# Hybrid streaming encoder step: weight splitting and modulation moved from GpSimd to VectorE, groups reordered, part of the modulation moved to the second feed-forward part

## The chip, the cores and the metric

The kernel runs on one core of a Trainium2 chip. The metric is the device time in microseconds of one execution of the whole program. The core's engines are TensorE (PE, with its weight loads as PEld), VectorE (DVE), ScalarE (ACT), GpSimd (POOL) and SyncE (SP), which issues all DMAs of this kernel. Each engine works through its own queue in order.

## The reference

One layer of an encoder is computed for 1024 prompt tokens and 32 sample tokens, model width 1024, feed-forward width 2816, all in float32.

```python
def layer(x, c, ...):
    mod = silu(c) @ w_mod + b_mod                    # (1024) @ (1024, 9*1024), for two c: prompt and sample
    sh1, sc1, g1, sh2, sc2, g2, sh3, sc3, g3 = split(mod, 9)
    h = rmsnorm(x, gains[0]) * (1 + sc1) + sh1
    x = x + 0.5 * g1 * rmsnorm((silu(h @ w1_gate) * (h @ w1_up)) @ w1_down, gains[1])
    h = rmsnorm(x, gains[2]) * (1 + sc2) + sh2
    qa, ka, va, qb, kb, vb = split(h @ w_in)
    o = concat([rmsnorm(band_attention_A), rmsnorm(window_attention_B)]) @ w_out
    x = x + g2 * rmsnorm(o, gains[3])
    h = rmsnorm(x, gains[4]) * (1 + sc3) + sh3
    x = x + 0.5 * g3 * rmsnorm((silu(h @ w2_gate) * (h @ w2_up)) @ w2_down, gains[5])
    return x, (new keys and values)
```

## The kernel before

**Stages.** The 1056 tokens are cut into three blocks: block 0 and block 1 of 384 tokens, block 2 of 288 (256 prompt tokens and the 32 sample tokens). The kernel runs the first feed-forward part (key `h1`, "part one"), then the projections, both attentions and the output projection, then the second feed-forward part (key `h3`, "part two"). Activations lie with the model dimension on the partitions and tokens along the free dimension.

**Precision.** Every float32 matrix product is made of three matmuls in a reduced format. `pair_of` splits a weight tile of 128 x 512: ScalarE writes the rounded copy `w[:, 0]` (line 549), another engine subtracts it from the original to get the remainder `w[:, 1]` (line 550). The three products are high x high, high x low, low x high (`product`, line 609, and `down`, lines 821 to 823).

**Groups and rounds.** The 22 slices of the feed-forward width make 11 groups of two slices. A round is one group on some of the blocks: stages gate ("g"), up ("u") and down ("d"). `rounds` lists them, and the stages are interleaved so that gate of the next round comes ahead of down of this one. In part one before, groups 0 to 7 run on all three blocks, then 8 to 10 on blocks 0 and 1, then 8 to 10 again on block 2. In part two, groups 0 and 1 run on each block by itself (six single rounds, `LEAD = 2`), then 2 to 10 on all three.

**Plain groups and block products.** A plain group (`plain`) takes 8 products of weight quarters by activation halves for blocks 0 and 1 (four per block) and four for block 2. A "fast" group (`strassen`) treats gate or up on blocks 0 and 1 as a 2 x 2 block product and needs seven products in place of eight; block 2's four products ride along with four of the weights. For this it needs sums of weight quarters, S1 to S4 (`Mat.of`, line 574, tiles `ws`), with their own splits, and combinations of the activations, T1 to T4 (`combos`, lines 620 to 655). In part one before, groups 5 to 10 on blocks 0 and 1 are fast (`PLAIN = 5`); in part two, all three-block rounds are.

**GpSimd's share.** Before, GpSimd makes S1 to S4 (`SUMS_POOL`) and the remainders of their splits. In rounds on one block ("alone", `shared`) it also makes the remainders of A12 and A22 and of the second slice of down's weights (`Rows`, lines 550 and 601).

**Modulation.** The first 16 of 72 columns of 128 are made at the start with matmuls. The rest comes in pieces of three columns (`mod_aside`): for each of eight slices of the contraction, VectorE accumulates the prompt's product (`acc[0]`, lines 250 and 252). For the sample, ScalarE scales the slice (line 253), and GpSimd adds (lines 256 and 258). At the end small matmuls with a vector of ones sum over the partitions (line 265, tile `pms`), and VectorE adds the bias and forms coefficients. A piece has eleven steps.

**Order of the work.** Side work (norms, modulation, bias rows, combinations) stands in a list of generators, and `step(n)` advances the first of them n steps: five after each product group of a plain round in part one (`STEPS`), two after each of a fast one (`pace`), one after each pair of down's outputs. `need` runs side work until a named piece is done. This gives the program order, and a scheduler with a timeline model then orders each engine's instructions with that order as priority. `per_group` is a hook that `ffn` calls after each up stage, and also after each stage of round 0 in part one; `mod_rest` uses it to begin the modulation and the bias rows. In round 0 it runs after gate and after down, so both are begun twice, one after the other:

```python
            if what == "u" or (key, r) == ("h1", 0):
                if 2 in blocks:
                    per_group(gi)
```

**Buffers.** Tiles come from pools with fixed numbers of buffers: `w` (split weights), `r` (raw weights), `s` (slices such as `sl`, `ut`, `macc`), `g`, `ux`; `FFN1` and `FFN2` list the numbers for the two parts. The pool `h` has five buffers for `ws`, for the modulation's loads `wma` and scaled slices `wmn`, and for the norms' temporaries.

Of the kernel before, what the change touches and what calls it, by code (L numbers as in the profile page):

```python
# [55 lines left out]
START = "x02nw1y3"  # L56
LEAD = 2
LAST = 3
PLAIN = 5
STEPS = {"h1": (5, 5), "h3": (6, 6)}  # L60
FFN1 = {"ux": 3, "r": 4, "w": 4, "g": 6, "s": 11}
FFN2 = {"ux": 3, "r": 4, "w": 5, "g": 6, "s": 9}
MIX = {"w": 8, "r": 3, "g": 5, "s": 5, "m": 1}
MODS = [(("ux", 6), ("r", 2))] * 4
SUMS_POOL = ("S1", "S2", "S3", "S4")
ZPOOL = (1, 0, 1, 0)
LATE = 1
PRIME = 0
# [16 lines left out]
def encoder_step(ctx: ExitStack, tc, x_prompt, x_sample, cache_a_k, cache_a_v, cache_b_k, cache_b_v,  # L85
# [152 lines left out]
    def mod_aside(c0, nc_):  # L238

        w = 128 * nc_  # L240
        acc = [s_tile([128, 384], "macc")[:, :w] for _ in range(2)]
        for g in range(4):
            r = h_tile([128, 2, 384], "wma")[:, :, :w]
            dma.dma_start(r, w_mod[0, 256 * g:256 * (g + 1), 128 * c0:128 * c0 + w]
                          .rearrange("(k p) n -> p k n", p=128))
            n = h_tile([128, 2, 384], "wmn")[:, :, :w]
            for kk in range(2):
                k = 2 * g + kk
                if k == 0:
                    ve.tensor_scalar(acc[0], r[:, kk], csil[:, k, 0:1], None, op0=OP.mult)  # L250
                else:
                    ve.scalar_tensor_tensor(acc[0], r[:, kk], csil[:, k, 0:1], acc[0], op0=OP.mult, op1=OP.add)  # L252
                ae.activation(n[:, kk], r[:, kk], AF.Copy, scale=csil[:, k, 1:2])  # L253
                if kk:
                    to = acc[1] if g == 0 else n[:, 0]
                    ge.tensor_tensor(to, n[:, 0], n[:, 1], op=OP.add)  # L256
                    if g:
                        ge.tensor_tensor(acc[1], acc[1], n[:, 0], op=OP.add)  # L258
                yield
        yield  # L260
        yield
        pm = pc("pms")[:, :2 * nc_].rearrange("p (j b) -> p j b", j=2)
        for j in range(2):
            for b in range(nc_):
                te.matmul(pm[:, j, b:b + 1], acc[j][:, 128 * b:128 * b + 128], ones, start=j == 0 and b == 0,
                          stop=j == 1 and b == nc_ - 1, skip_group_check=True)
        ve.tensor_copy(modT[:, :, c0:c0 + nc_], pm)
        coefs(c0, c0 + nc_)
        yield

    def mod_all(first):
        for c0 in range(first, 72, 3):
            yield from mod_aside(c0, min(3, 72 - c0))


    ub = {}
# [266 lines left out]
        yield from norm_h(f, tb, j + 1, H)  # L543


    def pair_of(src, tag="w", at=None, by=None):

        w = at if at is not None else t_tile(tag, [128, 2, 4, 128], "w", F32R)
        ae.activation(w[:, 0], src, AF.Copy)  # L549
        (by or ve).tensor_tensor(w[:, 1], src, w[:, 0], op=OP.subtract)  # L550
        return w[:, 0], w[:, 1]

    class Mat:


        def __init__(self, wm, gi, shared):
            self.aside = ("A12", "A22") if shared else ()
            self.r = []
            for d in range(2):
                r = t_tile("r", [128, 4, 256], "raw")  # L560
                dma.dma_start(r, wm[0, 512 * d:512 * d + 512, 256 * gi:256 * gi + 256]
                              .rearrange("(k p) n -> p k n", p=128))
                self.r.append(r)
            self.a = {f"A{f + 1}{d + 1}": self.r[d][:, :, 128 * f:128 * f + 128] for f in range(2) for d in range(2)}
            self.done, self.places = {}, []

        def of(self, name):
            a = self.a
            if name not in a:
                x, y, op = {"S1": ("A21", "A22", OP.add), "S2": ("S1", "A11", OP.subtract),  # L570
                            "S3": ("A11", "A21", OP.subtract), "S4": ("A12", "S2", OP.subtract)}[name]
                x, y = self.of(x), self.of(y)
                a[name] = h_tile([128, 4, 128], "ws")
                (ge if name in SUMS_POOL else ve).tensor_tensor(a[name], x, y, op=op)  # L574
            return a[name]

        def split(self, name):
            if name not in self.done:
                self.done[name] = pair_of(self.of(name), *(self.places.pop(0) if self.places else ()),
                                          by=ge if name[0] == "S" or name in self.aside else ve)  # L580
            return self.done[name]

    class Rows:


        def __init__(self, wm, gi, tag, shared):
            self.raw, self.w, self.tag, self.shared = [], {}, tag, shared
            for ff in (2 * gi, 2 * gi + 1):
                r = t_tile("r", [128, KT, 128], "raw")
                dma.dma_start(r, wm[0, 128 * ff:128 * ff + 128, :].rearrange("p (k n) -> p k n", n=128))  # L590
                self.raw.append(r)

        def split(self, q, hf):
            if (q, hf) in self.w:
                return
            if self.tag == "w":
                self.w[q, hf] = pair_of(self.raw[q][:, 4 * hf:4 * hf + 4], by=ge if self.shared and q else ve)
                return
            t = t_tile(self.tag, [128, 2, KT, 128], "wd", F32R)
            ae.activation(t[:, 0], self.raw[q], AF.Copy)  # L600
            (ge if self.shared and q else ve).tensor_tensor(t[:, 1], self.raw[q], t[:, 0], op=OP.subtract)
            for h in range(2):
                self.w[q, h] = t[:, 0, 4 * h:4 * h + 4], t[:, 1, 4 * h:4 * h + 4]

# [57 lines left out]
    def rounds(key):  # L662
        both, n = (0, 1, 2), NF // 2
        if key == "h3":
            return [(g, (tb,)) for tb in both for g in range(LEAD)] + [(g, both) for g in range(LEAD, n)]
        return [(g, both) for g in range(n - LAST)] + [(g, (0, 1)) for g in range(n - LAST, n)] + \
            [(g, (2,)) for g in range(n - LAST, n)]

    STRASSEN = [("A11", "B11", "a", 2), ("A12", "B21", "a", 2), ("S2", "T2", "b", 0), ("S1", "T1", "d", 0),
                ("S3", "T3", "b", 0), ("A22", "T4", "e", 2), ("A21", None, None, 2), ("S4", "B22", "d", 0)]  # L670
# [1 line left out]
    def ffn(key, H, tags, F, facc, wg, wu, wd, per_group, key_out, after, beside=lambda: None):  # L672
# [2 lines left out]
        final = {tb: max(i for i, (g, t) in enumerate(plan) if tb in t) for tb in range(3)}  # L675
        T, sl, gs, loaded = {}, {}, {}, {}
        pace = 2
        fast = {r for r, (g, t) in enumerate(plan) if len(t) == 3 and (key == "h3" or g >= PLAIN) or len(t) == 2}
        stages = []
        for r, (gi, blocks) in enumerate(plan):  # L680
            held = [stages.pop()] if r else []
# [2 lines left out]
        def load(i):  # L684
            if i >= len(stages) or stages[i] in loaded:
                return
            r, what = stages[i]
            gi, blocks = plan[r]
            alone = len(blocks) == 1
            if what == "d":  # L690
                loaded[r, what] = Rows(wd, gi, "ux" if key == "h1" and alone else "w", alone)
            else:
                loaded[r, what] = Mat((wg, wu)[what == "u"], gi, alone)

        def ready(i):

# [141 lines left out]
        yield  # L838
        if key == "h3":
            begin((key, 2), between(F2[2], 2, 1, H3))  # L840
            begin((key, "T"), combos(H, T, tags))
        for i, (r, what) in enumerate(stages):
            gi, blocks = plan[r]
            if (key, r, what) == ("h1", 0, "u"):
# [23 lines left out]
            elif r == 0 and key == "h1":  # L868
                mu = loaded[r, "u"]
                mu.places = [(None, p) for p in wide()] + [("r",)]  # L870
                for tb in blocks:
                    need((key, tb))
                    last = tb == blocks[-1]
                    plain(r, "g", m, [tb], lambda n: None)
                    plain(r, "u", mu, [tb], lambda n, last=last: nexts(n, 1, i + 1) if last else None)
            elif r in fast:
                need((key, "T"))
                strassen(r, what, m, 2 in blocks, lambda n: nexts(n, 4 if what == "g" else 5))
            else:
                for tb in blocks:  # L880
                    need((key, tb))
                if what == "g" and (key, gi) == ("h1", PLAIN - 1):
                    begin((key, "T"), combos(H, T, tags), first=True)
                plain(r, what, m, blocks, lambda n: nexts(n, 2 * len(blocks) - 1))
            if what == "u" or (key, r) == ("h1", 0):
                if 2 in blocks:
                    per_group(gi)
                if gi == NF // 2 - 1:
                    beside()

# [28 lines left out]
    F1 = [None] * 3  # L919
    H2, H3 = [None] * 3, [None] * 3  # L920

    def mod_rest(gi):
        if gi == 0:
            in_order.close()
            begin("mod", mod_all(16))
            begin("bias", bias_rows())

    ffn1 = ffn("h1", H1, (("T3", "ux"), ("T1", "u"), ("T2", "ux"), ("T4", "u")), F1, lambda tb: u_tile(tb, "facc", F32), w1_gate, w1_up, w1_down, mod_rest, "h2",
# [688 lines left out]
    def facc2(tb):  # L1617
        return u_tile(tb, "facc", F32) if tb else pools["ux"].tile([128, KT, 384], F32, name="facc", tag="ux")

    for _ in ffn("h3", H3, (("T3", "ux"), ("T1", "x"), ("T2", "ux"), ("T4", "x")), F3, facc2, w2_gate, w2_up, w2_down, lambda gi: None, "y", finale, beside):  # L1620
        pass
    finish()

# [26 lines left out]
```

## Time and profile before

| | |
|---|---|
| median of 3 runs | 2368.66 us (2366.12 to 2372.91) |
| profiled execution: time | 2369.16 us |
| profiled execution: span, first to last instruction | 2367.4 us |
| mean granted TensorE clock | 0.959 |
| part one, first gate matmul to last down matmul | 43 to 967 us |
| part two, first gate matmul to end | 1555 to 2367 us |

In the profile's rows, L550 is line 550 of the kernel; a group's row gives line, engine, operation, tiles (written <- read), shape, count, busy time, mean duration in ns, and the idle time ahead of it with what ended it. A row of windows gives start and end, width, then busy time and number of instructions of each engine, the granted clock as a share of full speed, the DMA engines' busy share and GB/s. A row of waits names who waited for whom, with the sum, the number and the longest. A row of the chain or the timeline begins with the start and the length in us.

### The profile page before, as it was taken

To read this page: it belongs to the slowest core of one execution; us is meant where nothing else is said; L and a number is where in the kernel's file an instruction comes from. 1 tells how busy PE (TensorE), PEld (TensorE's weight loads), DVE (VectorE), ACT (ScalarE), POOL (GpSimd) and SP (SyncE) were. 2 spreads that over 40 slices of the span, in tenths; PEclk is the share of its full clock that TensorE was granted. 3 is DMA by queue.
4 is the path that set the end of the run, shared out by engine and by line. 5 is a ranking of instruction groups with operands and counts; after the bars stand their busy time and mean duration, and the time that the engine had idled before them with its cause. 6 is when DMAs were issued, how large, how long until landed. Compare 5 with 4: busy or idle time off the path is not lost.

```text
span 2367.4 us, 36544 instructions
## 1 busy us (share of the span) xinstructions
PE 2197.4 (93%) x13988; PEld 2083.5 (88%) x13988; DVE 1572.6 (66%) x2891; ACT 1010.4 (43%) x2118; POOL 928.3 (39%) x850
## 2 busy tenths in 40 slices
PE   7999989998889998889999999985999999999998
PEld 4999989998888898889978768985999999999997
DVE  5688898777878658767754576678535455545548
ACT  4464433434434334447654566344442232323224
POOL 2275563566667534310011032345462333333321
PEclk8999999999999999889999989997999999999999
DMA  8355435333433334410121211152431111111114
GB/s 318 102 161 165 136 123 157 107 102 117 133 98 121 121 94 147 145 56 25 30 57 28 65 37 54 54 164 90 126 106 37 54 54 54 49 42 46 45 54 129
DMA packets 179123, 225.05 MB, mean 95 GB/s; under 512 B 10116, under 2 KB 162116, under 8 KB 177796
## 3 DMA queue, kind: packets, MB, share of 16 engines
q1 hardware_dynamic: 178948, 222.71, 30.5%
q8 instruction: 110, 1.80, 0.3%
q14 instruction: 65, 0.53, 0.1%
HBM read 202.94 MB, written 26.03 MB: 97 GB/s over the span
## 4 chain that ended last, share of the span: by engine, by line
PE 63%; DVE 19%; DMA 7%; POOL 4%; issue 3%; ACT 2%; SPq 0%; DVEq 0%; POOLq 0%; ACTq 0%
PE gu L609 7%; PE ge L609 6%; DVE macc L252 5%; PE dn L821 5%; PE dn L822 5%; PE dn L823 5%; PE up L609 5%; PE gate L609 4%; PE g L609 4%; DMA wma<-in_w_mod_dram 4%; PE po L1003 2%; PE S L1042 2%; PE pq L352 2%; DVE w L550 2%; PE pq L354 2%
## 5 line engine op out<-in xcount | busy, mean ns | idle before, releaser
L550 DVE TENSOR_TENSOR w<-raw,w 128x512 fp32r<-128x512 f32 x279 | 259.6, 933 | 211.1 <-ACT w L549 209.8
L821 PE MATMUL dn<-gg,w 128*128 128x384 f32 (+1 forms) x1008 | 335.0, 333 | 37.0 <-ACT facc L826 18.6
L549 ACT ACTIVATE w<-raw 128x512 fp32r<-128x512 f32 x327 | 202.6, 629 | 354.7 <-PE gu L609 111.4
L822 PE MATMUL dn<-gg,w 128*128 128x384 f32 (+1 forms) x1008 | 329.1, 326 | 2.0 <-DVE gg L724 2.0
L823 PE MATMUL dn<-gg,w 128*128 128x384 f32 (+1 forms) x1008 | 328.6, 326 | 0.0
L828 DVE TENSOR_TENSOR facc<-dn,facc 128x768 f32<-128x768 f32 (+1 forms) x240 | 212.1, 886 | 148.7 <-PE dn L823 148.7
L550 POOL TENSOR_TENSOR w<-ws,w 128x512 fp32r<-128x512 f32 x120 | 169.0, 1415 | 287.3 <-ACT w L549 268.7
L252 DVE SCALAR_TENSOR_TENSOR macc<-wma,csil,macc 128x384 f32<-128x384 f32 (+1 forms) x266 | 245.2, 922 | 47.2 <-DMA wma<-in_w_mod_dram 43.4
L253 ACT ACTIVATE wmn<-wma,csil 128x384 f32<-128x384 f32 (+1 forms) x304 | 168.2, 604 | 177.4 <-DMA wma<-in_w_mod_dram 135.2
L821 PEld LDWEIGHTS dn<-gg,w 128*128 128x128 f32 x1008 | 192.4, 191 | 44.7 <-DVE facc L828 19.6
L609 PE MATMUL gu<-t,w 128*128 128x384 f32 x1080 | 207.0, 343 | 9.0 <-DVE sl L769 7.7
L256 POOL TENSOR_TENSOR wmn<-wmn 128x384 f32<-128x384 f32 (+1 forms) x114 | 126.8, 1112 | 199.0 <-ACT wmn L253 172.7
L609 PEld LDWEIGHTS gu<-t,w 128*128 128x128 f32 x1080 | 192.8, 194 | 11.0 <-DVE sl L769 8.3
L822 PEld LDWEIGHTS dn<-gg,w 128*128 128x128 f32 x1008 | 192.7, 191 | 2.4 <-DVE gg L724 2.4
L823 PEld LDWEIGHTS dn<-gg,w 128*128 128x128 f32 x1008 | 192.5, 191 | 0.0
L609 PE MATMUL g<-h_hi,w 128*128 128x288 f32 x768 | 164.7, 295 | 1.3 <-DVE facc L828 1.3
L574 POOL TENSOR_TENSOR ws<-raw 128x512 f32<-128x512 f32 x60 | 88.7, 1478 | 147.6 <-DMA raw<-in_w_up_dram 77.8
L258 POOL TENSOR_TENSOR macc<-macc,wmn 128x384 f32<-128x384 f32 (+1 forms) x114 | 135.4, 1188 | 7.1
L549 ACT ACTIVATE w<-ws 128x512 fp32r<-128x512 f32 x120 | 74.0, 629 | 149.7 <-PE gu L609 56.9
L609 PE MATMUL ge<-h,w 128*128 128x384 f32 x720 | 137.9, 335 | 0.0
L609 PE MATMUL gate<-h,w 128*128 128x384 f32 x672 | 125.0, 341 | 8.5 <-DVE w L550 5.1
L609 PEld LDWEIGHTS g<-h_hi,w 128*128 128x128 f32 x768 | 127.8, 188 | 2.0 <-DVE facc L828 1.7
(301 smaller groups left out, 5237.4 us busy)
## 6 DMA issues: line engine op xcount, KB each, us to landing
wma<-in_w_mod_dram SPq DMA_DIRECT2D x144, 384.0 KB, 3.3
raw<-in_w_gate_dram SPq DMA_DIRECT2D x58, 512.0 KB, 4.1
raw<-in_w_up_dram SPq DMA_DIRECT2D x58, 512.0 KB, 4.0
raw<-in_w_down_dram SPq DMA_DIRECT2D x58, 512.0 KB, 4.3
raw<-in_w_in_dram SPq DMA_DIRECT2D x18, 512.0 KB, 4.0
raw<-in_w_out_dram SPq DMA_DIRECT2D x13, 512.0 KB, 4.3
wm<-in_w_mod_dram SPq DMA_DIRECT2D x8, 768.0 KB, 11.2
xr<-xs SPq DMA_DIRECT2D x16, 384.0 KB, 4.0
```

Source lines behind the costliest of these rows:

```text
L252: ve.scalar_tensor_tensor(acc[0], r[:, kk], csil[:, k, 0:1], acc[0], op0=OP.mult, op1=OP.add)
L253: ae.activation(n[:, kk], r[:, kk], AF.Copy, scale=csil[:, k, 1:2])
L256: ge.tensor_tensor(to, n[:, 0], n[:, 1], op=OP.add)
L258: ge.tensor_tensor(acc[1], acc[1], n[:, 0], op=OP.add)
L549: ae.activation(w[:, 0], src, AF.Copy)
L550: (by or ve).tensor_tensor(w[:, 1], src, w[:, 0], op=OP.subtract)
L574: (ge if name in SUMS_POOL else ve).tensor_tensor(a[name], x, y, op=op)
L609: te.matmul(ps, w[a][:, k, :], x[b][k], start=first and k == 0 and q == 0, stop=last and k == n - 1 and q == 2, skip_group_check=True)
L821: te.matmul(ps[:, s, :w], h[:, k % 4, :], g[:, 0, :w], start=q == 0, stop=False)
L822: te.matmul(ps[:, s, :w], h[:, k % 4, :], g[:, 1, :w], start=False, stop=False)
L823: te.matmul(ps[:, s, :w], l[:, k % 4, :], g[:, 0, :w], start=False, stop=q == 1)
L828: ve.tensor_tensor(o, ps[:, :, :w], o, op=OP.add)
```

## The change

- GpSimd no longer takes part in the splitting of weights: S1 to S4 and all remainders are made by VectorE (`SUMS_POOL`, `shared` and `by` are gone).
- In `mod_aside`, VectorE accumulates both the prompt's and the sample's products, 16 instructions a piece; ScalarE's scaling and GpSimd's additions are gone, and with them the tile `wmn`.
- Part one's rounds become: groups 0 to 2 on blocks 0 and 1, groups 3 to 10 on all blocks, then groups 0 to 2 on block 2. Groups 0 to 6 are plain (`PLAIN = 7`), 7 to 10 use block products with block 2.
- The hook is called with the round's number. Part one makes the modulation's columns 16 to 63; the last eight (the gate of part two) begin in part two after the up stage of round 6.
- In part two the combinations T1 to T4 begin with round 4, block 2's first single, and no longer at the part's start. Its pools have four `w` and eleven `s` buffers.

```diff
-PLAIN = 5
+PLAIN = 7
-FFN2 = {"ux": 3, "r": 4, "w": 5, "g": 6, "s": 9}
+FFN2 = {"ux": 3, "r": 4, "w": 4, "g": 6, "s": 11}
-SUMS_POOL = ("S1", "S2", "S3", "S4")
...
-            n = h_tile([128, 2, 384], "wmn")[:, :, :w]
             for kk in range(2):
                 k = 2 * g + kk
-                if k == 0:
-                    ve.tensor_scalar(acc[0], r[:, kk], csil[:, k, 0:1], None, op0=OP.mult)
-                else:
-                    ve.scalar_tensor_tensor(acc[0], r[:, kk], csil[:, k, 0:1], acc[0], op0=OP.mult, op1=OP.add)
-                ae.activation(n[:, kk], r[:, kk], AF.Copy, scale=csil[:, k, 1:2])
-                if kk:
-                    to = acc[1] if g == 0 else n[:, 0]
-                    ge.tensor_tensor(to, n[:, 0], n[:, 1], op=OP.add)
-                    if g:
-                        ge.tensor_tensor(acc[1], acc[1], n[:, 0], op=OP.add)
+                for j in range(2):
+                    c = csil[:, k, j:j + 1]
+                    if k == 0:
+                        ve.tensor_scalar(acc[j], r[:, kk], c, None, op0=OP.mult)
+                    else:
+                        ve.scalar_tensor_tensor(acc[j], r[:, kk], c, acc[j], op0=OP.mult, op1=OP.add)
                 yield
...
-    def mod_all(first):
-        for c0 in range(first, 72, 3):
+    def mod_all(first, last):
+        for c0 in range(first, last, 3):
...
-        (by or ve).tensor_tensor(w[:, 1], src, w[:, 0], op=OP.subtract)
+        ve.tensor_tensor(w[:, 1], src, w[:, 0], op=OP.subtract)
...
-                (ge if name in SUMS_POOL else ve).tensor_tensor(a[name], x, y, op=op)
+                ve.tensor_tensor(a[name], x, y, op=op)
...
-            (ge if self.shared and q else ve).tensor_tensor(t[:, 1], self.raw[q], t[:, 0], op=OP.subtract)
+            ve.tensor_tensor(t[:, 1], self.raw[q], t[:, 0], op=OP.subtract)
...
-        return [(g, both) for g in range(n - LAST)] + [(g, (0, 1)) for g in range(n - LAST, n)] + \
-            [(g, (2,)) for g in range(n - LAST, n)]
+        return [(g, (0, 1)) for g in range(LAST)] + [(g, both) for g in range(LAST, n)] + \
+            [(g, (2,)) for g in range(LAST)]
...
-        fast = {r for r, (g, t) in enumerate(plan) if len(t) == 3 and (key == "h3" or g >= PLAIN) or len(t) == 2}
+        fast = {r for r, (g, t) in enumerate(plan) if len(t) == 3 and (key == "h3" or g >= PLAIN)}
...
             begin((key, 2), between(F2[2], 2, 1, H3))
-            begin((key, "T"), combos(H, T, tags))
...
-                if what == "g" and (key, gi) == ("h1", PLAIN - 1):
-                    begin((key, "T"), combos(H, T, tags), first=True)
+                if what == "g" and (key, r) in (("h1", PLAIN - 1), ("h3", 2 * LEAD)):
+                    begin((key, "T"), combos(H, T, tags), first=key == "h1")
...
-                if 2 in blocks:
-                    per_group(gi)
+                per_group(r)
...
-    def mod_rest(gi):
-        if gi == 0:
+    def mod_rest(r):
+        if r == 0:
             in_order.close()
-            begin("mod", mod_all(16))
+            begin("mod", mod_all(16, 64))
             begin("bias", bias_rows())
...
+    def beside_lead(r):
+        if r == 3 * LEAD:
+            begin("mod", mod_all(64, 72))
```

More of the change, by code (lines that the diff above doesn't have):

```diff
@@ L269, in mod_aside @@
         yield
-    def mod_all(first):
-        for c0 in range(first, 72, 3):
-            yield from mod_aside(c0, min(3, 72 - c0))
+    def mod_all(first, last):
+        for c0 in range(first, last, 3):
+            yield from mod_aside(c0, min(3, last - c0))
     ub = {}
@@ L543, in between, with pair_of, __init__ @@
         yield from norm_h(f, tb, j + 1, H)
-    def pair_of(src, tag="w", at=None, by=None):
+    def pair_of(src, tag="w", at=None):
         w = at if at is not None else t_tile(tag, [128, 2, 4, 128], "w", F32R)
         ae.activation(w[:, 0], src, AF.Copy)
-        (by or ve).tensor_tensor(w[:, 1], src, w[:, 0], op=OP.subtract)
+        ve.tensor_tensor(w[:, 1], src, w[:, 0], op=OP.subtract)
         return w[:, 0], w[:, 1]
     class Mat:
-        def __init__(self, wm, gi, shared):
-            self.aside = ("A12", "A22") if shared else ()
+        def __init__(self, wm, gi):
             self.r = []
@@ L578, in split, with __init__ @@
             if name not in self.done:
-                self.done[name] = pair_of(self.of(name), *(self.places.pop(0) if self.places else ()),
-                                          by=ge if name[0] == "S" or name in self.aside else ve)
+                self.done[name] = pair_of(self.of(name), *(self.places.pop(0) if self.places else ()))
             return self.done[name]
     class Rows:
-        def __init__(self, wm, gi, tag, shared):
-            self.raw, self.w, self.tag, self.shared = [], {}, tag, shared
+        def __init__(self, wm, gi, tag):
+            self.raw, self.w, self.tag = [], {}, tag
             for ff in (2 * gi, 2 * gi + 1):
@@ L596, in split @@
             if self.tag == "w":
-                self.w[q, hf] = pair_of(self.raw[q][:, 4 * hf:4 * hf + 4], by=ge if self.shared and q else ve)
+                self.w[q, hf] = pair_of(self.raw[q][:, 4 * hf:4 * hf + 4])
                 return
@@ L688, in load @@
             gi, blocks = plan[r]
-            alone = len(blocks) == 1
             if what == "d":
-                loaded[r, what] = Rows(wd, gi, "ux" if key == "h1" and alone else "w", alone)
+                loaded[r, what] = Rows(wd, gi, "ux" if key == "h1" and len(blocks) == 1 else "w")
             else:
-                loaded[r, what] = Mat((wg, wu)[what == "u"], gi, alone)
+                loaded[r, what] = Mat((wg, wu)[what == "u"], gi)
         def ready(i):
@@ L1618, in facc2 @@
         return u_tile(tb, "facc", F32) if tb else pools["ux"].tile([128, KT, 384], F32, name="facc", tag="ux")
-    for _ in ffn("h3", H3, (("T3", "ux"), ("T1", "x"), ("T2", "ux"), ("T4", "x")), F3, facc2, w2_gate, w2_up, w2_down, lambda gi: None, "y", finale, beside):
+    def beside_lead(r):
+        if r == 3 * LEAD:
+            begin("mod", mod_all(64, 72))
+    for _ in ffn("h3", H3, (("T3", "ux"), ("T1", "x"), ("T2", "ux"), ("T4", "x")), F3, facc2, w2_gate, w2_up, w2_down, beside_lead, "y", finale, beside):
         pass
```

## The prediction

> **What bounds the kernel now.** I read the page first, then the windows by stage, then the engines' waits, then the timeline of VectorE beside GpSimd.
>
> ```profile
> PE 2197.4 (93%) x13988; PEld 2083.5 (88%) x13988; DVE 1572.6 (66%) x2891; ACT 1010.4 (43%) x2118; POOL 928.3 (39%) x850
> PEclk8999999999999999889999989997999999999999
> ```
>
> TensorE is busy 93% of 2367.4 us, so at most some 7% can be won by better feeding. The windows, cut at the ends of rounds, say where it is lost: width, then busy us of PE (with its matmuls), PEld, DVE, ACT, POOL, then clock.
>
> ```profile
> 43.00:133.00 90.00, 84.42 (x528) 82.28 (x528) 68.41 (x138) 47.94 (x99) 34.44 (x32) 0.94 0.44 139
> 133.00:171.00 38.00, 33.31 (x202) 32.79 (x201) 31.23 (x40) 22.67 (x40) 25.74 (x23) 0.96 0.53 156
> 171.00:256.00 85.00, 79.75 (x507) 77.20 (x506) 77.31 (x103) 40.81 (x77) 52.24 (x45) 1.00 0.53 161
> 256.00:345.00 89.00, 82.84 (x512) 82.05 (x512) 76.44 (x108) 39.42 (x77) 52.16 (x46) 0.94 0.46 141
> 345.00:424.00 79.00, 75.69 (x469) 74.73 (x468) 66.62 (x122) 28.01 (x52) 37.62 (x28) 0.98 0.42 126
> 424.00:503.00 79.00, 73.62 (x461) 72.42 (x459) 56.67 (x81) 32.11 (x61) 40.20 (x35) 0.98 0.35 111
> 503.00:587.00 84.00, 75.38 (x455) 73.04 (x455) 64.46 (x93) 35.07 (x66) 55.00 (x45) 0.96 0.38 113
> 587.00:671.00 84.00, 75.27 (x461) 72.96 (x459) 64.08 (x90) 35.92 (x68) 54.33 (x45) 0.96 0.38 113
> 671.00:748.00 77.00, 68.98 (x405) 67.58 (x406) 61.80 (x86) 32.18 (x61) 53.29 (x43) 0.93 0.41 125
> 748.00:810.00 62.00, 53.78 (x275) 51.70 (x274) 45.36 (x90) 20.77 (x40) 38.38 (x31) 0.89 0.43 132
> 895.00:967.00 72.00, 61.79 (x426) 60.53 (x424) 60.08 (x97) 31.41 (x52) 35.33 (x23) 0.91 0.43 144
> 1616.00:1657.00 41.00, 16.13 (x69) 15.30 (x68) 35.74 (x63) 17.69 (x37) 17.07 (x11) 0.63 0.16 54
> 1833.00:1899.00 66.00, 64.92 (x409) 64.60 (x408) 32.79 (x46) 18.21 (x35) 23.14 (x16) 1.00 0.17 49
> ```
>
> The last row is one round of block products in part two. It takes 66.0 us. The same round in part one (503 to 748) takes 77 to 84 us, and there POOL and DVE are far busier and the clock is lower. What TensorE itself needs comes from undisturbed runs of matmuls in the chain, the first on 384 columns, the second on 288, the third one modulation piece:
>
> ```profile
> 864.16 4.16 PE gu L609 x24
> 1899.26 3.19 PE g L609 x24
> 176.75 1.23 PE pms L265 x12
> ```
>
> So 0.173 us for 384 columns, 0.133 for 288, and 0.480 for one product on all three blocks. A plain round has 96 products per block for gate and up and 48 for down: 144 x 0.480 = 69.1 us. A round of block products has 168 at 0.173, 96 at 0.133 and 48 at 0.480: 64.9 (the row above: 66.0). Without block 2 it is 45.7, a plain round on blocks 0 and 1 is 49.9, block 2 alone 19.1.
>
> Part one before, 43 to 967 us: five plain rounds, three of block products, three with two blocks and three singles need 345 + 195 + 137 + 57 = 734 us, and 38 modulation pieces 47. Of 924 us about 140 are lost: near 36 up to 171 (rounds 0 and the gate of 1), 33 from 171 to 503 (four plain rounds, and 221 further matmuls, some 18 pieces: 299 needed), 40 from 503 to 748 (205 needed), 24 from 748 to 967 (195 needed).
>
> Why, the timeline of 20 us shows; DVE first, then POOL:
>
> ```profile
> 699.81 0.55 DVE L724 TENSOR_TENSOR gg<-sl,gg 128x384 fp32r<-128x384 f32 x1
> 700.28 0.61 DVE L252 SCALAR_TENSOR_TENSOR macc<-wma,csil,macc 128x384 f32<-128x384 f32 x1
> 705.22 1.49 DVE L550 TENSOR_TENSOR w<-raw,w 128x512 fp32r<-128x512 f32 x1
> 706.63 1.63 DVE L252 SCALAR_TENSOR_TENSOR macc<-wma,csil,macc 128x384 f32<-128x384 f32 x1
> 713.45 0.61 DVE L252 SCALAR_TENSOR_TENSOR macc<-wma,csil,macc 128x384 f32<-128x384 f32 x1
> 713.98 0.16 DVE L267 COPY modT<-pms 128x6 f32<-128x6 f32 x1
> 714.51 0.68 DVE L550 TENSOR_TENSOR w<-raw,w 128x512 fp32r<-128x512 f32 x1
> 715.11 1.37 DVE L252 SCALAR_TENSOR_TENSOR macc<-wma,csil,macc 128x384 f32<-128x384 f32 x1
> 717.76 0.94 DVE L828 TENSOR_TENSOR facc<-dn,facc 128x768 f32<-128x768 f32 x1
> 718.63 1.19 DVE L252 SCALAR_TENSOR_TENSOR macc<-wma,csil,macc 128x384 f32<-128x384 f32 x1
> 705.05 1.11 POOL L258 TENSOR_TENSOR macc<-macc,wmn 128x384 f32<-128x384 f32 x1
> 706.12 1.72 POOL L550 TENSOR_TENSOR w<-ws,w 128x512 fp32r<-128x512 f32 x1
> ```
>
> With POOL silent (713.45, 714.51) the accumulation takes 0.61 and the weights' remainder 0.68; beside a POOL instruction (705.22, 706.63) they take 1.49 and 1.63. Starts stand closer than durations: 0.53 us after the accumulation, 0.60 after the remainder, 0.47 after a 384-wide subtraction, 0.87 after the sum out of PSUM (717.76 to 718.63). [...]
>
> ```profile
> L252 DVE SCALAR_TENSOR_TENSOR macc<-wma,csil,macc 128x384 f32<-128x384 f32 (+1 forms) x266 | 245.2, 922 | 47.2 <-DMA wma<-in_w_mod_dram 43.4
> L253 ACT ACTIVATE wmn<-wma,csil 128x384 f32<-128x384 f32 (+1 forms) x304 | 168.2, 604 | 177.4 <-DMA wma<-in_w_mod_dram 135.2
> L258 POOL TENSOR_TENSOR macc<-macc,wmn 128x384 f32<-128x384 f32 (+1 forms) x114 | 135.4, 1188 | 7.1
> PE pms L265 <- DVE macc L252: 12.3, 5, 4.5
> PE pms L265 <- DVE macc L252: 12.0, 5, 4.2
> PE gu L609 <- POOL w L550: 6.7, 8, 1.5
> PE dn L821 <- ACT facc L826: 18.6, 2, 15.3
> ```
>
> The waits are TensorE's: the first two in 100 to 500 and 500 to 900 us, the third in the rounds of part two, the last in its lead. The 304 activations are 38 pieces of eight: the hook that starts the modulation is called twice in round 0, so every piece is made twice. After, it is 2 x 16 in part one and 3 in part two, 35.
>
> **The change, part by part.**
>
> *Matmuls of part one.* Seven plain groups (three split into two blocks and one) and four with block products need 3 x (49.9 + 19.1) + 4 x 69.1 + 4 x 64.9 = 743 us, 8 more than before. Six fewer pieces give 6 x 1.23 = 7 back, and three return in part two (+3.7). So TensorE's need stays near 782 us in part one; only the losses can move.
>
> *Modulation on VectorE.* A piece was 8 accumulations on DVE, 8 activations, 7 POOL sums; it becomes 16 DVE instructions. At a pitch of 0.53 that is 8.5 us, with the small ones 8.8. The 30 pieces that the hand-counted steps put into rounds 1 to 6 (eleven steps each; 366 steps there after those for the combinations, 36 of them for the bias rows) are 264 us. The DMA waits of 43 us should mostly go, since a piece no longer takes two of the five h buffers per load. [...]
>
> *DVE in rounds 1 to 6.* A plain round: 12 remainders x 0.60, 12 products and remainders of 0.47 (narrow ones 3/4), 12 sums of 0.87 (narrow 3/4) = 22 us; with two blocks 18. Rounds 1 to 6: 2 x 18 + 4 x 22 + 264 + combinations (20 wide instructions x 0.87, and some 8 us behind the POOL sums that stay) 25 + bias 6 = 419 us. TensorE needs there 2 x 49.9 + 4 x 69.1 + 30 x 1.23 = 413. Two queues are equally loaded, which is the weak point: it can't run at 413. Bounds: 419 with no friction; 332/299 = 1.11 of TensorE's need, as rounds 1 to 4 ran before, gives 458. DVE was busy up to 77.3 of 85 us there, 91%; 419/0.92 = 455. I take 455, a loss of 42, near the upper bound because the pieces' small matmuls still stand in TensorE's order and wait for the accumulators.
>
> *Rounds 7 to 10.* The modulation is out by the start of round 7. DVE has the 32.8 us of the 1833 row, 16 instructions more at 0.60 (10), less what POOL held up: some 40 of 65. Each takes 66.0; round 7 with two late pieces 69. Before, 171 to 748 lost 73 us; after, rounds 1 to 7 lose 42 + 2: 29 won. Rounds 8 to 10 and the singles lost 24, half of it from 748 to 810 with modulation still running; I take 15: 9 won. At the start only blocks 0 and 1 must be normed for round 0: of 36 lost I take 4 back (bounds 0 and the 14 us in which block 2's products stood there). Part one: 42 less 1.
>
> [...]
>
> *Part two.* Sums and remainders on DVE take the 6.7 us of POOL waits away. The third modulation part is 12 loads on SP's queue ahead of weights, 24 + 24 DVE instructions (25 us, covered: DVE is half idle) and 3.7 us of TensorE. The combinations start with block 2's first single instead of right behind its norm. In the 1616 row TensorE is busy 16 of 41 us, with ACT's copy out of PSUM (15.3 us wait) behind ACT's norm and combinations; the norm remains, the combinations (some 14 of the 41) move under two rounds of TensorE work of 38 us. I take 5 (bounds 0 and 14). Weights with 4 buffers instead of 5: nothing, since part one's block products ran on 4 with the waits named above; at worst each of 18 stages waits for one copy and remainder, 18 x 1.3 = 24. Sum: 3.7 - 6.7 - 5 = -8.
>
> *Sum.* The profiled execution took 2369.2 (span 2367.4), 0.5 above the median. 2369.2 - 41 - 8 = 2320.
>
> **The rivals.**
>
> *VectorE becomes the bound (slower).* Accumulations in a row that depend on each other start 0.65 us apart in the chain:
>
> ```profile
> 297.19 0.63 DVE macc L252
> 297.84 0.63 DVE macc L252
> 298.50 0.63 DVE macc L252
> ```
>
> If the two accumulators don't alternate cleanly, a piece costs 16 x 0.12 = 1.9 us more, 30 of them 58; DVE needs 477, at 92% 518, and part one's gain of 41 turns into a loss of 22: 2369.2 + 22 - 8 = 2383. It decides from a pitch of 0.62. Against it: the new loop alternates them, so each has another between. [...]
>
> *The stalls were never POOL's (same).* In-order queues lose as much without POOL, part one keeps its 924 us: 2369.2 - 6.7 + 3.7 = 2366. For it: DVE's busy time in part one hardly falls (contention out, work in). Against: the 1833 row.
>
> [...]
>
> **How the numbers follow.** Forecast 0.45, DVE-bound 0.17, same 0.13, port 0.20, something else 0.05, split. Within 0.3% (7 us, about what this kernel's runs can tell apart) lies the second rival: 0.14. Slower 0.19, faster 0.67. Range 2284 to 2374: from the third rival to short of the first, which with the unknown is left out; the forecast's own range is 2300 to 2345.
>
> **What the profile after would show.** L252 near 0.62 us mean, not 0.92, and x480 to x500; no POOL row of L256, L550 or L574 left; rounds 3 to 6 near 76 us each and 7 to 10 near 66, clock 1.00; part one's last down near 926 instead of 967. Wrong: PE's waits for macc L252 above 24 us and DVE over 95% busy in the plain rounds (first rival); rounds of 77 to 84 us with POOL silent (second); weights' waits in part two's rounds (four buffers).

## The result

The changed kernel takes 2305.15 us (median of 4 runs, 2302.55 to 2307.05) against 2369.16 (4 runs, 2366.12 to 2372.91): 64 us less, ratio 0.9728 with a 95% interval of 0.9711 to 0.9746. The forecast was 2320, with a range of 2284 to 2374. The profiled execution's span fell from 2367.4 to 2300.6 us.

The page after, first its busy shares, then the clock in forty slices:

```profile
PE 2176.9 (95%) x14004; PEld 2070.8 (90%) x14004; DVE 1611.4 (70%) x3383; ACT 843.6 (37%) x1800; POOL 214.6 (9%) x293
PEclk9999999998999998999999999999999999999999
```

VectorE is busier than before (1611 us against 1573) and executes 492 instructions more; GpSimd fell from 928 to 215 us. The groups of the modulation and of the weights after:

```profile
L252 DVE SCALAR_TENSOR_TENSOR macc<-wma,csil,macc 128x384 f32<-128x384 f32 (+1 forms) x490 | 279.6, 611 | 4.8 <-DMA wma<-in_w_mod_dram 4.8
L544 DVE TENSOR_TENSOR w<-raw,w 128x512 fp32r<-128x512 f32 x333 | 231.0, 703 | 96.2 <-ACT w L543 94.4
```

490 accumulations cost 280 us, 266 had cost 245: the mean fell from 922 to 611 ns. The waits for their loads fell from 43 to 5 us. Nine of them in a row show the distance from start to start, 4.84 less 0.61 us over eight steps, 0.53:

```profile
160.26 4.84 DVE L252 SCALAR_TENSOR_TENSOR macc<-wma,csil,macc 128x384 f32<-128x384 f32 x9
```

The windows after, cut at the ends of down's rounds; columns as before:

```profile
42.50:131.00 88.50, 82.94 (x488) 81.05 (x487) 75.63 (x175) 41.94 (x83) 13.43 (x14) 0.94 0.52 176
131.00:192.00 61.00, 60.80 (x370) 60.48 (x368) 55.55 (x115) 13.02 (x25) 0.00 (x0) 1.00 0.57 170
192.00:259.00 67.00, 65.62 (x409) 64.35 (x410) 62.96 (x131) 11.04 (x21) 0.00 (x0) 1.00 0.58 175
259.00:343.00 84.00, 79.47 (x498) 78.69 (x498) 69.33 (x168) 15.09 (x29) 0.00 (x0) 0.98 0.57 175
343.00:423.00 80.00, 77.93 (x507) 77.15 (x505) 63.80 (x133) 13.08 (x26) 0.00 (x0) 1.00 0.45 139
423.00:505.00 82.00, 76.77 (x479) 76.21 (x478) 79.25 (x128) 16.37 (x29) 15.25 (x6) 0.96 0.35 107
505.00:588.00 83.00, 78.19 (x465) 75.95 (x464) 74.26 (x178) 17.22 (x33) 0.00 (x0) 0.92 0.50 152
588.00:655.00 67.00, 65.44 (x412) 65.23 (x411) 39.11 (x63) 18.92 (x35) 0.00 (x0) 1.00 0.17 48
655.00:724.00 69.00, 66.90 (x412) 66.70 (x411) 39.16 (x63) 18.84 (x36) 0.00 (x0) 0.98 0.16 47
1887.00:1956.00 69.00, 66.59 (x410) 66.38 (x409) 39.07 (x62) 18.64 (x34) 0.00 (x0) 0.98 0.16 46
```

The plain rounds 3 to 6 take 80 to 84 us with VectorE busy up to 79 of 82; block products in part one take 67 to 69 us, and 77 to 84 before. The last row is one round of part two: it was 66.0 us before and is 69 now.

The table shows where the 67 us of span come from. The stages are cut at TensorE instructions of the timeline: part one begins with the first gate matmul, and the cuts behind it are its last down matmul, the first scores of mixer B, the first gate matmul of part two, its first block product, its last down matmul and the end.

| stage, us | before | after | difference | forecast |
|---|---|---|---|---|
| part one | 924.4 | 874.6 | -49.8 | -41 |
| from part one to the first scores | 89.2 | 78.7 | -10.5 | 0 |
| attention and output projection | 499.1 | 496.1 | -3.0 | 0 |
| part two's lead, the single rounds | 178.8 | 153.4 | -25.4 | -5 |
| part two's rounds of block products | 614.0 | 637.6 | +23.6 | -3 |
| end | 19.0 | 17.6 | -1.4 | 0 |

So the sum was near, but two of its terms were far off and stood against each other.

### The profile page after: what moved, and what is told of

It reads as the page before. It is cut to its first block, busy times and chain, and to the rows that moved or that the text cites. A ratio compares the mean times of both kernels' runs of the same rounds, so it can differ in the third digit from the quotient of the medians.

```text
span 2300.6 us, 35729 instructions
## 1 busy us (share of the span) xinstructions
PE 2176.9 (95%) x14004; PEld 2070.8 (90%) x14004; DVE 1611.4 (70%) x3383; ACT 843.6 (37%) x1800; POOL 214.6 (9%) x293
## 4 chain that ended last, share of the span: by engine, by line
PE 74%; DVE 14%; DMA 5%; issue 4%; ACT 2%; POOL 1%; SPq 1%; DVEq 0%; ACTq 0%; POOLq 0%
PE gu L601 8%; PE up L601 7%; PE gate L601 6%; PE ge L601 6%; PE dn L812 6%; PE dn L813 6%; PE dn L814 6%; PE g L601 5%; DVE w L544 3%; DVE macc L252 3%; PE po L992 2%; PE S L1031 2%; PE pq L346 2%; DMA raw<-in_w_up_dram 2%; PE pq L348 2%
## 5 line engine op out<-in xcount | busy, mean ns | idle before, releaser
L544 DVE TENSOR_TENSOR w<-raw,w 128x512 fp32r<-128x512 f32 x333 | 231.0, 703 | 96.2 <-ACT w L543 94.4
L252 DVE SCALAR_TENSOR_TENSOR macc<-wma,csil,macc 128x384 f32<-128x384 f32 (+1 forms) x490 | 279.6, 611 | 4.8 <-DMA wma<-in_w_mod_dram 4.8
L601 PE MATMUL gu<-t,w 128*128 128x384 f32 x936 | 175.3, 340 | 1.0 <-DVE w L544 1.0
L601 PE MATMUL gate<-h,w 128*128 128x384 f32 x864 | 161.7, 342 | 9.0 <-DVE w L544 7.3
L601 PEld LDWEIGHTS gate<-h,w 128*128 128x128 f32 x864 | 152.0, 191 | 11.2 <-DVE w L544 8.6
L389 POOL TENSOR_TENSOR sq<-sq 128x384 f32<-128x384 f32 (+1 forms) x48 | 52.3, 1099 | 1146.3 <-ACT sq L385 1134.2
L601 PE MATMUL up<-h,w 128*128 128x384 f32 x792 | 146.3, 337 | 1.1 <-ACT w L543 1.1
L601 PEld LDWEIGHTS up<-h,w 128*128 128x128 f32 x792 | 137.4, 189 | 2.3 <-ACT w L543 2.2
L714 ACT ACTIVATE gg<-sl 128x384 fp32r<-128x384 f32 (+1 forms) x132 | 62.4, 492 | 195.5 <-DVE sl L713 194.8
L601 PE MATMUL g<-h_lo,w 128*128 128x288 f32 x416 | 122.7, 295 | 0.0
```

The source lines that it names most:

```text
L252: ve.scalar_tensor_tensor(acc[j], r[:, kk], c, acc[j], op0=OP.mult, op1=OP.add)
L389: e.tensor_tensor(sq[:, 0, :w], sq[:, 0, :w], sq[:, 1, :w], op=OP.add)
L544: ve.tensor_tensor(w[:, 1], src, w[:, 0], op=OP.subtract)
L601: te.matmul(ps, w[a][:, k, :], x[b][k], start=first and k == 0 and q == 0, stop=last and k == n - 1 and q == 2, skip_group_check=True)
L714: ae.activation(g[:, 0, :w], v, AF.Copy)
```

## The experiments

Medians are compared with the kernel before on the same chip; the stages are those of the table above.

**The three parts alone.** Each starts from the kernel before.

```diff
# o1_mod_dve: modulation
-                ae.activation(n[:, kk], r[:, kk], AF.Copy, scale=csil[:, k, 1:2])
-                if kk: ... ge.tensor_tensor(...)
+                for j in range(2):
+                    ... ve.scalar_tensor_tensor(acc[j], r[:, kk], c, acc[j], op0=OP.mult, op1=OP.add)
# o2_weights_dve: sums and remainders of weights
-SUMS_POOL = ("S1", "S2", "S3", "S4")
+SUMS_POOL = ()
-... by=ge if name[0] == "S" or name in self.aside else ve
+... by=ve
# o3_order: part one's rounds
-PLAIN = 5
+PLAIN = 7
-        return [(g, both) for g in range(n - LAST)] + ...
+        return [(g, (0, 1)) for g in range(LAST)] + [(g, both) for g in range(LAST, n)] + [(g, (2,)) for g in range(LAST)]
... (which rounds are fast, and the hook's argument, follow as in the change)
```

Expected of the modulation alone:

> The kernel before with one part of the change: the modulation's pieces accumulate on VectorE alone (16 instructions a piece, no ScalarE scaling, no GpSimd sums). GpSimd keeps its weights; order and part two stay. Port theory (GpSimd's instructions holding VectorE are what part one loses): GpSimd's 308 us of modulation sums go, part one shortens by 25 to 40 us, L252's mean falls from 0.92 to below 0.75 us: 2335. Order theory (what counts is that the modulation is out before the block products and that block 2's first groups come last): VectorE still works on it in the block products' rounds, at most 10 us: 2362.

Measured: 2330.81 us against 2366.22, ratio 0.9852 (0.9838 to 0.9867), 35 us won, 34 of them in part one (890.5). Its accumulations, with GpSimd still busy with weights:

```profile
L253 DVE SCALAR_TENSOR_TENSOR macc<-wma,csil,macc 128x384 f32<-128x384 f32 (+1 forms) x532 | 327.5, 660 | 2.8 <-DMA wma<-in_w_mod_dram 2.8
```

The mean is 660 ns, not 922, below the 0.75 us of the port theory. VectorE took over half of the modulation and part one got shorter. The row shows a second difference: VectorE's waits for the modulation's loads are 2.8 us here and 43.4 before, and the likely reason is that the scaled slices `wmn` no longer take buffers of the pool `h`.

Expected of the weights alone:

> The kernel before with one part of the change: all sums and remainders of weights on VectorE; modulation, order and part two's buffers as before. Port theory: in part one GpSimd keeps 308 of some 450 us, so 5 to 15 us are won there; in part two GpSimd falls silent, and if its work was only in the way, rounds of 65.6 us become 65. Queue theory (VectorE, in order, now stands waiting for the up weights with the sums out of PSUM behind): part two's rounds grow to 66.5 to 69 us, 10 to 20 us in all. Port alone: 2355; queue as well: 2370.

Measured: 2348.32 us against 2366.22, ratio 0.9928 (0.9913 to 0.9943), 18 us won. Part one gained only 2.6, so the 5 to 15 forecast there didn't come, although the accumulations got faster:

```profile
L252 DVE SCALAR_TENSOR_TENSOR macc<-wma,csil,macc 128x384 f32<-128x384 f32 (+1 forms) x266 | 227.1, 854 | 39.1 <-DMA wma<-in_w_mod_dram 35.6
```

The lead gained 4.0. Part two's rounds fell from 614.0 to 605.5: the queue theory is wrong for this kernel, which has five `w` buffers in part two. One stretch of its part two:

```profile
1833.00:1899.00 66.00, 66.00 (x417) 65.92 (x416) 39.89 (x64) 18.65 (x35) 0.00 (x0) 1.00 0.16 49
```

TensorE is busy 66.00 of 66.00 us with VectorE doing all the weights.

Expected of the order alone:

> The kernel before with part one's order alone: groups 0 to 2 on blocks 0 and 1 first and on block 2 last, seven plain groups, four of block products; GpSimd keeps weights and modulation, all modulation stays in part one, part two unchanged. Order theory: start 15 us shorter, modulation out before the block products: 2335. Port theory: 8 us more matmuls and the same instructions held up, only the start gains: 2362.

Measured: 2360.40 us against 2366.22, ratio 0.9980 (0.9968 to 0.9991), 6 us won, near the port theory's 2362, but not at its place: part one did not change (924.9), and the stretch from part one to the first scores fell from 89.2 to 79.4. With GpSimd at work, the accumulations are as slow as ever:

```profile
L252 DVE SCALAR_TENSOR_TENSOR macc<-wma,csil,macc 128x384 f32<-128x384 f32 (+1 forms) x266 | 249.7, 939 | 25.2 <-DMA wma<-in_w_mod_dram 21.6
```

The three alone sum to 59 us; all together won 64, with part two's own edits in it.

**VectorE's load in the plain rounds.** From the changed kernel, with the hook that starts modulation and bias rows called once:

```diff
-            if what == "u" or (key, r) == ("h1", 0):
+            if what == "u" or (key, r, what) == ("h1", 0, "g"):
```

> The changed kernel, but the modulation and the bias rows are begun once in round 0 and not twice (16 pieces in part one in place of 32). If VectorE's load is what holds the plain rounds at 80 to 84 us against 69 of matmuls: 141 us of VectorE and 20 us of TensorE go, rounds 3 to 6 take 70 to 72 us, 2255. If the rounds are held by waits for weights or for PSUM that are there anyway: only the pieces' matmuls, 2285.

Measured: 2260.40 us against 2366.22, ratio 0.9555 (0.9540 to 0.9569), by the two ratios 41 us below the changed kernel (span 2259.9 against 2300.6). Part one takes 831.8 us, 43 less. Its windows just before and after the modulation ends at 303 us:

```profile
259.00:330.00 71.00, 66.64 (x417) 65.38 (x416) 66.50 (x139) 18.33 (x31) 18.92 (x6) 0.98 0.44 132
330.00:400.00 70.00, 70.00 (x439) 70.00 (x438) 23.40 (x34) 13.89 (x26) 0.00 (x0) 1.00 0.15 46
```

In the second VectorE is busy 23 of 70 us and TensorE all of the time, with 439 matmuls in 70 us (a plain round has 432). So plain rounds of 80 to 84 us were held by the modulation, TensorE's share of it (16 x 1.23 = 20 us) and VectorE's.

The last gate's pieces put back into part one load the same queue from the other side:

```diff
-            begin("mod", mod_all(16, 64))
+            begin("mod", mod_all(16, 72))
-            begin("mod", mod_all(64, 72))
+            pass
```

> The changed kernel with the last gate's modulation (columns 64 to 71) back in part one, where it is made twice: six more pieces there, three fewer in part two. If the plain rounds are bound by VectorE's load: part one +45 to +60 us (six pieces of 8.8 us on a queue that is full), part two -4 to -10: 2350. If the modulation drains into the block products' rounds, where VectorE is half idle: part one +8 (six times 1.23 us of TensorE), 2305.

Measured: 2318.56 us against 2372.86, ratio 0.9781 (0.9752 to 0.9810), 13 us above the changed kernel's 2305. Neither number came. Part one is 896.3, 22 more for six pieces, 3.6 us each and not 8.8: the pieces ran on until 680 us, into the first two rounds of block products, where VectorE has room for them (it is busy 39 of 67 us there without them). Part two's rounds gained 6.4, inside the 4 to 10.

**Part two's rounds.** The changed kernel with part two's pools as before:

```diff
-FFN2 = {"ux": 3, "r": 4, "w": 4, "g": 6, "s": 11}
+FFN2 = {"ux": 3, "r": 4, "w": 5, "g": 6, "s": 9}
```

> The changed kernel with part two's pools as before (five w buffers, nine s instead of four and eleven). Buffer theory (with four, the gate's last remainders come late, the raw buffers they read come free late, and the up weights land when their sums are already due): part two's rounds, 638 us from the first block product to the last down matmul, fall to 610 to 615, 2280. Queue theory (VectorE, in order, waits for the up weights whatever the buffers) or modulation theory (the third modulation part in part two costs it): rounds stay near 635, 2303.

Measured: 2279.77 us against 2372.86, ratio 0.9614 (0.9586 to 0.9642). The rounds fall from 637.6 to 609.7 us, the buffer theory's number. The edit also takes two `s` buffers away; that a smaller pool made the rounds shorter is unlikely, but no run changes the one without the other. How four buffers cost a stall can be read in one round of the changed kernel: SyncE's loads of up, ScalarE's copy, VectorE's remainder and sums, TensorE's wait.

```profile
1913.21 2.46 SPq L554 DMA_DIRECT2D raw<-in_w_up_dram  x2
1913.91 0.63 ACT L543 ACTIVATE w<-raw 128x512 fp32r<-128x512 f32 x1 [1.45 <-PE gu L601]
1914.57 0.69 DVE L544 TENSOR_TENSOR w<-raw,w 128x512 fp32r<-128x512 f32 x1 [0.17 <-ACT w L543]
1920.17 0.69 DVE L567 TENSOR_TENSOR ws<-raw 128x512 f32<-128x512 f32 x1 [4.90 <-DMA raw<-in_w_up_dram]
1924.98 0.55 DVE L760 TENSOR_TENSOR sl<-gu,sl 128x384 f32<-128x384 f32 x1
1925.68 3.88 PE L601 MATMUL gu<-h,w 128*128 128x384 f32 x12 [2.41 <-DVE sl L760]
```

The gate's last remainder (1914.57) waits for ScalarE's half, and ScalarE (1913.91) waited 1.45 us for TensorE to be done with a `w` buffer; only then is the raw buffer free (all that SyncE waits for in this stretch are such remainders), and the second load of up goes out at 1915.3. VectorE stands 4.9 us for it, since the sums are next in its queue: a remainder whose copy ScalarE had ended at 1918.2 runs at 1920.78, behind the first sum. The sums out of PSUM (L760) come behind them, and TensorE waits 2.4 us for the PSUM tile that they free. With five buffers, in 65 us (the length of a round) of the same kernel otherwise, the loads, VectorE's wait and the window:

```profile
1901.41 4.05 SPq L554 DMA_DIRECT2D raw<-in_w_up_dram  x2
```

```profile
DVE ws L567 <- DMA raw<-in_w_up_dram: 1.7, 1, 1.7
```

```profile
1900.00:1965.00 65.00, 65.00 (x410) 64.92 (x409) 39.60 (x64) 18.48 (x35) 0.00 (x0) 1.00 0.16 49
```

The wait is 1.7 us and TensorE doesn't see it. Over all the rounds of block products in part two the changed kernel's largest wait is this, and the one with five buffers has none of the kind:

```profile
PE gu L601 <- DVE sl L760: 14.0, 7, 2.4
```

All the rounds in one window, first the changed kernel, then the one with five buffers:

```profile
1645.40:2283.00 637.60, 618.64 (x3892) 614.20 (x3891) 394.87 (x662) 193.19 (x352) 7.88 (x9) 0.99 0.21 61
1647.90:2257.60 609.70, 608.12 (x3866) 605.37 (x3865) 393.31 (x651) 188.79 (x347) 7.92 (x9) 1.00 0.20 62
```

TensorE is idle 19 us in the first and 2 in the second; the other 10.5 us are longer busy time for the same matmuls, at a mean clock of 0.99 against 1.00.

**Part two's lead.** The changed kernel with the combinations at the start of part two, as before:

```diff
+            begin((key, "T"), combos(H, T, tags))
-                if what == "g" and (key, r) in (("h1", PLAIN - 1), ("h3", 2 * LEAD)):
+                if what == "g" and (key, r) == ("h1", PLAIN - 1):
```

> The changed kernel with part two's combinations begun at the start of the part, as before. If their move is what shortened the lead of part two (179 to 153 us, against 5 us forecast): lead back to 172 to 178, 2325. If it was the weights' remainders leaving GpSimd: lead stays near 155, 2305.

Measured: 2331.67 us against 2372.86, ratio 0.9828 (0.9797 to 0.9858). The lead is 178.8 us again, exactly the value before. Its wait is back as well, the longest of TensorE's in the lead:

```profile
PE dn L812 <- ACT facc L817: 15.3, 1, 15.3
```

The window around it, and below it the window at the same place of the lead in the changed kernel:

```profile
1550.00:1600.00 50.00, 25.98 (x121) 24.77 (x122) 42.58 (x73) 23.12 (x46) 18.02 (x13) 0.72 0.20 65
```

```profile
1545.00:1595.00 50.00, 46.47 (x269) 45.31 (x268) 46.04 (x88) 27.75 (x58) 14.00 (x12) 1.00 0.41 129
```

In the changed kernel the longest wait in the lead is 4.5 us, for a weight's remainder. So all 25 us of the lead come from the combinations' place in the order. The whole lead, again first with the combinations early:

```profile
1497.00:1675.80 178.80, 147.54 (x849) 143.60 (x850) 128.29 (x230) 84.50 (x154) 34.19 (x25) 0.90 0.38 117
1492.00:1645.40 153.40, 141.34 (x849) 137.54 (x850) 123.96 (x230) 82.95 (x154) 40.02 (x25) 0.98 0.43 136
```

Of the 25 us, 19 are TensorE's idle time (31 against 12), and 6 are longer busy time for the same 849 matmuls, at a clock of 0.90 against 0.98.

**Put together.** First once, five buffers in part two, and PLAIN = 3, which makes all groups on three blocks block products:

> The changed kernel with modulation and bias rows begun once, five w and nine s buffers in part two, and four more groups as block products in part one (PLAIN = 3; only the three groups split between blocks stay plain). From 2260 of the once-begun one: 25 less by the buffers if the buffer theory holds, 17 less for 4 x 4.16 us of matmuls: 2219. Rival: with the modulation now beside block products VectorE is full again and part one gains nothing: 2235; buffers nothing as well: 2260.

Measured: 2245.40 us against 2372.86, ratio 0.9469 (0.9442 to 0.9496): 26 above the forecast. Part two's rounds gave the 25 (610.4), part one nothing: 840.6 against 831.8 with PLAIN = 7, although it has 16.6 us less of matmuls. Its first two rounds of block products took 77 us each, with modulation in them until 386 us, near the rival's account; the later ones took 67 to 69 us, as in the changed kernel, which also has four `w` buffers in part one. So part one got five:

```diff
-FFN1 = {"ux": 3, "r": 4, "w": 4, "g": 6, "s": 11}
+FFN1 = {"ux": 3, "r": 4, "w": 5, "g": 6, "s": 9}
```

> The changed kernel with five w and nine s buffers in both parts. From 2280 with part two's buffers alone: if four buffers also cost part one's four rounds of block products (67 to 69 us each) 2 to 4 us a round: 2268. If part one is bound by VectorE and not by buffers, or misses the two s buffers: 2280 or more.

Measured: 2252.62 us against 2365.29, ratio 0.9523 (0.9509 to 0.9537); part one 853.1 in place of 876.7. Twice the forecast: besides the block products, which now leave TensorE no gap,

```profile
560.00:760.00 200.00, 200.00 (x1265) 199.77 (x1265) 123.96 (x228) 56.83 (x105) 0.00 (x0) 1.00 0.21 64
```

the other rounds gained as well: round 6 ends at 578 us in place of 591. This edit, too, goes back to nine `s` buffers. With modulation begun once, and seven, five and four plain groups:

> The same with modulation and bias rows begun once. From the two effects measured alone (2260 with once, 26 less by part two's buffers) 2234; with part one's block products at 65 us in place of 67 to 69, 2224.

> The same with five plain groups (PLAIN = 5): two more groups as block products, 2 x 4.16 us of matmuls less, 2216 if the block products in part one run at TensorE's 65 us; 2224 or more if the modulation beside them fills VectorE.

> The same with four plain groups (PLAIN = 4): 2212 if the trend holds; above the kernel with five where the combinations and the modulation's last pieces meet in the same round.

Measured against 2365.29: 2214.86 (ratio 0.9367, 0.9353 to 0.9381), 2206.56 (0.9328, 0.9313 to 0.9344) and 2214.44 (0.9361, 0.9347 to 0.9375). The first two came out 9 us below their forecasts (2224 and 2216), the third 2 above its 2212. Five plain groups are best, but not through part one, which takes 802.1 us with seven, 803.7 with five and 796.1 with four. The difference lies in the stretch from there to the first scores: 90.7, 81.2 and 90.4 us. In all the runs this stretch is either near 80 or near 90, and the sums of the norms on TensorE (`pss`) that stand in it go with that. Before, after, with seven and with five plain groups:

```profile
L384 PE MATMUL pss<-ones,sq 128*128 128x1 f32 (+1 forms) x36 | 4.5, 235 | 0.0
L378 PE MATMUL pss<-ones,sq 128*128 128x1 f32 (+1 forms) x24 | 2.7, 221 | 0.0
L378 PE MATMUL pss<-ones,sq 128*128 128x1 f32 (+1 forms) x36 | 4.1, 224 | 0.0
L378 PE MATMUL pss<-ones,sq 128*128 128x1 f32 (+1 forms) x24 | 2.7, 217 | 0.0
```

Where 36 of them are left behind the last down matmul, the stretch takes 89 to 91 us; where 24 to 27 are left, 77 to 81. So a part of the norms has slipped behind the end of part one in the slow cases. What decides whether it does was not settled. The kernel with five, 159 us below the kernel before, on its page:

```profile
PE 2120.5 (96%) x13764; PEld 2025.5 (92%) x13764; DVE 1513.3 (69%) x3096; ACT 852.5 (39%) x1820; POOL 211.4 (10%) x293
```

## Why the prediction was right, and where it wasn't

The total is nearer than its terms, and in part that is luck. In the profiled execution the six stages of the table miss their forecasts by -9, -10, -3, -20, +27 and -1 us.

**GpSimd held VectorE: right in the durations; what it is worth is not separated.** The accumulations' mean is 611 ns, 620 forecast, 490 of them; the modulation alone is worth 35 us, and the order without it leaves 939 ns. The rival that the stalls were never GpSimd's (2366) does not fit that pair. But the modulation's edit does two things at once: it quiets GpSimd, and it frees the buffers that the modulation's loads wait for. In the chain of part one that ended last, these loads hold 92 us before, 93 with the order alone and 17 with the modulation alone; the accumulations themselves hold 119, 134 and 105. The weights alone quiet GpSimd and leave the loads' waits (35.6 us on VectorE): the mean falls to 854 ns, and part one gains 2.6 us. So how the 34 us of part one divide between GpSimd's hold on VectorE and the loads stays open. The prediction named these loads as waits that go, but gave them no time of their own.

**VectorE nearly as full as TensorE in the plain rounds: right.** Rounds 1 to 6 were put at 455 us. From 131 to 588 us it took 457, a stretch that holds round 7's gate in place of round 1's, 4 us more of matmuls:

```profile
131.00:588.00 457.00, 438.79 (x2717) 432.82 (x2716) 405.16 (x850) 85.81 (x159) 15.25 (x6) 0.97 0.50 152
```

VectorE is busy 405 us there, 419 were forecast; at 0.89 of the time, and not the 0.92 that the sum used, it is less full than TensorE with 439. The list of signs named "near 76 us" for rounds 3 to 6, which the sum itself did not say: 455 less two rounds of 55 leaves 86 each, and 80 to 84 was measured. Begun once, the rounds behind the modulation take 70. Six more pieces cost 3.6 us each and not 8.8, so VectorE's queue is not the only bound. The DVE-bound rival's pitch of 0.65 did not come (0.53, above); the pieces' waits on TensorE, 24 us in 100 to 900 before, are these 3 in 500 to 900, and none stands among the waits of 100 to 500:

```profile
PE pms L259 <- DVE macc L252: 3.0, 3, 1.3
```

**The start: mis-sized.** Forecast 4 us, measured 14: from the first gate matmul to the end of round 0 it takes 88.5 us for 66.5 of matmuls, 22 lost, against 36. The order is the smaller part of it: with the order alone, round 0 ends at 139.4 us in place of 130.9 and loses 30, so 6 are won. With the modulation alone and the old order, round 0 ends 9 us sooner (161.8 for 171.2); the first pieces of modulation, from 108 us on, fall into this stretch. The prediction counted the order alone. All the rest of part one together gave 36 us for a forecast of 37; its rounds of block products took 67, 69 and 66 us for a forecast of 66.

**Between the parts: missing.** No term stood for the 10.5 us from part one to the first scores. The order alone gives 9.8 of them (79.4): 12 sums of the norms, and the waits around them, no longer stand behind the last down matmul. As two of the later runs have the new order and take 90 us again, the order does not assure it.

**The combinations' move: right in kind, wrong in size.** The wait of 15.3 us behind ScalarE was quoted, and its cause put half on the norm, which stays. The run with the move undone shows that nothing of it was the norm's: the whole stall and its low clock (0.72 in that window) went with the move, 25 us against 5. My upper bound of 14 was too low: it was the stretch that the combinations filled, while TensorE is busy 20 us less in the window of the stall (26.0 of 50 against 46.5), and runs at a lower clock there (0.72 against 1.00).

**"Weights with 4 buffers instead of 5: nothing": wrong.** It cost 28 us (637.6 to 609.7); the worst case in the prediction was 24. The reasoning was that part one ran on four with small waits; but part one's block products were slow for all reasons together, and that four buffers were one of them could not be read there. The undisturbed reference, part two's own rounds with five, was at hand. What failed was the step to the price, "each of 18 stages waits for one copy and remainder": the chain goes on from the remainder to the raw buffer, the next load, the sums on VectorE and the sums out of PSUM behind them. With GpSimd the wait for the load stood on a queue of its own (77.8 us of its waits on the page before are for loads of up). With five buffers the weights on VectorE are a gain of 8.5 us, near the 6.7 that the prediction took for the vanished waits.

**VectorE beside GpSimd.** The means of the same accumulation go with GpSimd's busy time: 922 and 939 ns where GpSimd is busy 509 and 480 us of part one (before and the order alone), 854 with 351 (the weights alone), 660 with 209 (the modulation alone), 616 with 56 (after). VectorE's sums out of PSUM, which have one input in PSUM, kept their mean: 886 ns before, 887 after. Why the one slows and the other doesn't, no run shows. "Port" in the chances and the expectations, and "the third rival" in the range, are the author's names for the theory that GpSimd's instructions hold VectorE; a port no run shows, these means are what the runs show. The pitch of 0.53 us that the forecast used was measured again, between accumulations that take 0.61; the total of 2305, with terms that missed both ways, would not decide it.

## What to carry to other kernels

Cost an engine's work by its start-to-start pitch where the neighbour is silent (here 0.53 us), not by its mean beside a busy one (0.92): VectorE took 1.8 times the accumulations (490 for 266) in 1.14 times the time. When a queue takes over work, follow the chain past the instruction to the buffer it frees, the load that waits for that buffer, and what stands behind the load's first reader. Count how often a block of side work is issued: here it was made twice, and beginning it once saved another 41 us.

## What the runs showed that was not expected

One buffer of split weights decides whether rounds run at TensorE's own pace: 28 us in part two, 24 in part one, with TensorE busy 200.00 of 200 us once it is there. And a stall of 15 us on one ScalarE copy stands in a lead that is 25 us longer: 19 us of this are idle time of TensorE, and 6 are the same 849 matmuls at a granted clock of 0.90 in place of 0.98.
